# Expert rows of 8 KB, fetched token rows, and one square root per group of queries

## The chip, the core and the metric

The kernel runs on one core of a Trainium2 chip. TensorE multiplies matrices from SBUF into PSUM, VectorE, ScalarE and GpSimd do the elementwise work, SyncE issues most DMAs, and 16 DMA engines carry the bytes. The metric is device time in microseconds (us). The median of three runs of the kernel before is 1703.13 us.

## What is computed

One layer of a diffusion backbone over 512 latent tokens and 256 context tokens, width 1024, in float32: a modulated normalisation, three token mixers in parallel (a gated linear recurrence, a gated short convolution, and attention with normalised queries and keys), their merge into the stream x, and then a mixture of 16 experts in which every expert chooses its 64 best tokens.

```python
def attend_latent(q, k_lat, v_lat, k_ctx, v_ctx):   # 16 heads of 64 over 4 key heads
    ...
def expert_choice_ffn(h, router_w, w_gate, w_up, w_down):
    bsz, n, d = h.shape
    cap = CAPACITY_FACTOR * n // N_EXPERTS
    aff = jax.nn.softmax((h @ router_w).astype(jnp.float32), axis=-1)
    w_sel, idx = lax.top_k(aff.transpose(0, 2, 1), cap)
    xs = jax.vmap(lambda hb, ib: hb[ib])(h, idx)
    hid = jax.nn.silu(jnp.einsum('becd,edf->becf', xs, w_gate)) * jnp.einsum('becd,edf->becf', xs, w_up)
    ys = jnp.einsum('becf,efd->becd', hid, w_down) * w_sel[..., None].astype(h.dtype)
    return jax.vmap(lambda yb, ib: jnp.zeros((n, d), h.dtype).at[ib.reshape(-1)].add(yb.reshape(-1, d)))(ys, idx)
def reference(...):
    ...
    q_l = apply_rope(rmsnorm(to_heads(pl[8], HEAD_DIM), q_norm_g), cos, sin)
    ...
    x = x + g_a * y_lat
    x = x + g_f * expert_choice_ffn(modulate(x, norm2_g[l], sh_f, sc_f), router_w[l], w_gate[l], w_up[l], w_down[l])
    return rmsnorm(x, final_norm_g)
```

The three expert matrices are 1024 x 1024 each, so 16 experts have 192 MiB of weights, which are read once.

## The kernel before

Dense products take three passes with activations and weights split into a high and a low part (lines 185 to 187). A Tile scheduler orders most work by priorities and its own model of time; in the attention units SyncE and TensorE run in the order of the code, and in the expert stage TensorE does (`manual_schedule`).

**Attention.** Four groups of four query heads. `queries(g, w)` forms a group's queries in two halves of 256 tokens: three-pass products (`tok_steps`), a sum of squares, a square root on ScalarE (line 582), a reciprocal and a product on VectorE, the rotation (`rope`, VectorE and GpSimd) and a split. `turn_keys` (line 562) and `turn_queries` (line 599) turn keys and queries by transposes on TensorE. 64 units follow, 16 to a group: `scores`, an exponential on ScalarE (line 623), `turn_probs` (line 632) and `values` (line 647). Between them a `Filler` gives each unit a share of dense steps: the next group's queries, and convolution columns, through which `mixed` strews the query turns. The square root and the exponential need different tables on ScalarE.

**From merge to experts.** The last dense product (`w_out`, lines 883 to 905) makes x1, four tiles of 128 tokens x 1024, and the router logits from its transposes (line 875). The expert stage begins with top-k on VectorE. `slot` tells each token's place in each expert.

**Experts.** They go in eight pairs, expert e on rows 64 e to 64 e + 63 of a tile. `wsrc` lists the loads: 1 MiB each, 256 rows of a matrix as two rows of 4 KB on each partition; the last pair's down matrices come in column blocks (`LASTC`) with rows of 1 KB and 512 bytes. `more` issues them on SyncE. The first 24 go into the slots of `ORDER` while earlier stages give memory back; then a ring of 20 slots is refilled, each chunk of matmuls freeing two (`refill`). A pair runs: gate and up in eight chunks (`pair_chunks`, line 1099), Silu and product into `hid` (lines 1139, 1140), `gather` of the next pair's tokens as 32 matmuls with a scaled one-hot matrix (line 1048) with evictions through VectorE and ScalarE (lines 1053, 1051), `weights` (line 1062), `scatter` of the pair before into the accumulator (lines 1085 to 1090), transposes of hid (line 1153), `by_slot` (line 1073), and four chunks of down. In the last pair the column blocks (line 1194) are added to x1 and normalised as they come.

## Time and profile before

| | |
|---|---|
| median of three runs | 1703.13 us (1701.49 to 1704.36) |
| profiled execution | 1698.42 us |
| its span | 1696.6 us |
| TensorE busy in the span | 1607.2 us (95%) |
| VectorE, ScalarE, GpSimd busy | 767.9, 527.7, 150.7 us |
| DMA | 305.52 MB, 180 GB/s in the mean |
| chain that ended last | TensorE 83%, VectorE 9%, ScalarE 5% |

Roughly: recurrence until 430 us, convolution, keys and values until 540, attention units until 815, merge and router until 1213, experts until the end. A busy TensorE is one with instructions in flight. All stretches are in us from the start of the span.

### The profile page before, as it was taken

To read this page: it belongs to the slowest core of one execution; us is meant where nothing else is said; L and a number is where in the kernel's file an instruction comes from. 1 tells how busy PE (TensorE), PEld (TensorE's weight loads), DVE (VectorE), ACT (ScalarE), POOL (GpSimd) and SP (SyncE) were. 2 spreads that over 40 slices of the span, in tenths; PEclk is the share of its full clock that TensorE was granted. 3 is DMA by queue.
4 is the path that set the end of the run, shared out by engine and by line. 5 is a ranking of instruction groups with operands and counts; after the bars stand their busy time and mean duration, and the time that the engine had idled before them with its cause. 6 is when DMAs were issued, how large, how long until landed. Compare 5 with 4: busy or idle time off the path is not lost.

```text
span 1696.6 us, 23600 instructions
## 1 busy us (share of the span) xinstructions
PE 1607.2 (95%) x9896; PEld 1207.7 (71%) x9896; DVE 767.9 (45%) x1173; ACT 527.7 (31%) x934; POOL 150.7 (9%) x142
## 2 busy tenths in 40 slices
PE   6999999999998899899999999999799999999996
PEld 4889898988898788788788888889244344444444
DVE  6364655556545666655646524343411222122124
ACT  4433324334225656654323223233010010011004
POOL 0021212222000000000000100110000000000005
PEclk9999999999999999999999999999899999999998
DMA  9410211122222000100555622348789999999995
GB/s 294 118 41 25 63 38 50 38 75 70 80 80 75 26 25 26 44 33 26 182 191 178 209 85 75 124 148 349 315 320 402 382 409 409 409 409 409 409 395 167
DMA packets 166287, 305.52 MB, mean 180 GB/s; under 512 B 6562, under 2 KB 115618, under 8 KB 164130
## 3 DMA queue, kind: packets, MB, share of 16 engines
q1 hardware_dynamic: 162624, 301.66, 48.9%
q10 hardware_dynamic: 3556, 2.35, 0.4%
q8 instruction: 78, 1.28, 0.3%
q14 instruction: 29, 0.24, 0.0%
HBM read 301.89 MB, written 2.10 MB: 179 GB/s over the span
## 4 chain that ended last, share of the span: by engine, by line
PE 83%; DVE 9%; ACT 5%; issue 2%; POOL 0%; DMA 0%; ACTq 0%; SPq 0%; DVEq 0%; POOLq 0%
PE d L185 14%; PE d L187 14%; PE d L186 14%; PE pg L1099 6%; PE pu L1099 6%; PE py L1099 6%; PE py L1048 3%; PE lv L304 2%; PE tp L647 2%; PE tp L632 2%; DVE wl L91 1%; PE mi L333 1%; PE sc L617 1%; PE sc L618 1%; ACT wh L90 1%
## 5 line engine op out<-in xcount | busy, mean ns | idle before, releaser
L185 PE MATMUL d<-hH,wh 128*128 128x512 f32 x640 | 257.2, 402 | 0.0
L187 PE MATMUL d<-hH,wl 128*128 128x512 f32 x640 | 253.4, 396 | 0.0
L186 PE MATMUL d<-hL,wh 128*128 128x512 f32 x640 | 252.4, 394 | 0.0
L91 DVE TENSOR_TENSOR wl<-raw,wh 128x2048 fp32r<-128x2048 f32 (+1 forms) x78 | 157.8, 2022 | 192.0 <-ACT wh L90 191.8
L90 ACT ACTIVATE wh<-raw 128x2048 fp32r<-128x2048 f32 (+1 forms) x78 | 128.9, 1652 | 218.2 <-PE d L186 167.4
L187 PEld LDWEIGHTS d<-hH,wl 128*128 128x128 f32 x640 | 121.0, 189 | 24.9
L185 PEld LDWEIGHTS d<-hH,wh 128*128 128x128 f32 x640 | 120.8, 189 | 22.3 <-issue 1.6
L186 PEld LDWEIGHTS d<-hL,wh 128*128 128x128 f32 x640 | 121.1, 189 | 21.3 <-issue 0.2
L1099 PE MATMUL pg<-mw,xT 128*64 128x512 f32 x512 | 115.6, 593 | 2.0 <-DVE xT L1053 2.0
L1099 PE MATMUL pu<-mw,xT 128*64 128x512 f32 x512 | 115.3, 592 | 0.0
L1099 PE MATMUL py<-mw,hT 128*64 128x512 f32 x448 | 97.7, 594 | 0.1
L315 POOL TENSOR_TENSOR kk<-kk,tt 128x384 f32<-128x384 f32 x56 | 77.0, 1376 | 190.8 <-DVE tt L317 143.6
L1099 PEld LDWEIGHTS pu<-mw,xT 128*64 128x64 f32 x512 | 36.7, 137 | 73.1 <-issue 72.8
L1099 PEld LDWEIGHTS pg<-mw,xT 128*64 128x64 f32 x512 | 36.1, 137 | 72.2 <-issue 68.8
L185 PE MATMUL d<-wh,hH 128*128 128x256 f32 x288 | 84.1, 292 | 0.0
L187 PE MATMUL d<-wh,hL 128*128 128x256 f32 x288 | 81.7, 284 | 0.0
L186 PE MATMUL d<-wl,hH 128*128 128x256 f32 x288 | 81.6, 283 | 0.0
L1140 DVE TENSOR_TENSOR hid<-hid,pu 128x1024 f32<-128x1024 f32 x8 | 9.8, 1221 | 154.4 <-PE pu L1099 148.0
L187 PE MATMUL d<-brh,wl 128*128 128x512 f32 x192 | 75.6, 396 | 2.6 <-DVE wl L91 2.6
L185 PE MATMUL d<-brh,wh 128*128 128x512 f32 x192 | 75.8, 396 | 1.7 <-ACT wh L90 1.5
L186 PE MATMUL d<-brl,wh 128*128 128x512 f32 x192 | 75.7, 396 | 0.0
L1099 PEld LDWEIGHTS py<-mw,hT 128*64 128x64 f32 x448 | 31.5, 137 | 60.8 <-issue 59.7
(354 smaller groups left out, 2998.1 us busy)
## 6 DMA issues: line engine op xcount, KB each, us to landing
mw<-in_w_gate_dram SPq DMA_DIRECT2D x64, 1024.0 KB, 18.2
mw<-in_w_up_dram SPq DMA_DIRECT2D x64, 1024.0 KB, 18.5
mw<-in_w_down_dram SPq DMA_DIRECT2D x62, 1024.0 KB, 17.4
raw<-in_w_in_dram SPq DMA_DIRECT2D x38, 1024.0 KB, 5.1
raw<-in_ada_w_dram SPq DMA_DIRECT2D x16, 1024.0 KB, 4.9
raw<-in_w_in_dram SPq DMA_DIRECT2D x24, 512.0 KB, 3.8
adaw<-in_ada_w_dram SPq DMA_DIRECT2D x8, 512.0 KB, 8.5
raw<-in_ada_w_dram SPq DMA_DIRECT2D x8, 512.0 KB, 7.8
```

The source lines that it names most:

```text
L90: act.activation(hi, src, AF.Copy)
L91: dve.tensor_sub(lo, src, hi)
L185: pe.matmul(p, lh(k), rh(k), start=k == 0, stop=False)
L186: pe.matmul(p, lh(k), rl(k), start=False, stop=False)
L187: pe.matmul(p, ll(k), rh(k), start=False, stop=k == KC - 1)
L304: pe.matmul(p[:, c], kc[:, c * 128:(c + 1) * 128], q_mix, start=True, stop=True)
L315: pool.tensor_mul(kb[:, :, 1], kb[:, :, 1], tb[:, :, 0, 0:1].to_broadcast([128, n2, m]))
L333: pe.matmul(pv[:, i], kt[:, i], v[:, c], start=True, stop=True)
L632: pe.transpose(tp[:, t], e[:, (t0 + t) * 128:(t0 + t + 1) * 128], ident)
L647: pe.matmul(av[hh * 64:hh * 64 + 64, i], va[:, t, g * 64:g * 64 + 64], pts[hh][:, t], start=t == 0, stop=t == 5)
L1048: pe.matmul(p[:, i], x1[:, t, (k0 + i) * 128:(k0 + i + 1) * 128], ohs[:, t], start=t == 0, stop=t == 3)
L1099: pe.matmul(dst[64 * e:64 * e + 64, hf_], src[:, k, 64 * e:64 * e + 64], wt[e][:, k2, hf_ * 512:hf_ * 512 + 512], start=k == 0, stop=k == ...
```

## The change

Six things change.

- **Expert rows.** A gate, up or down load (all but the last pair's column blocks) puts two neighbouring matrix rows on one partition, one run of 8 KB instead of two of 4 KB. The contracted index is thereby interleaved, so everything that multiplies it takes columns with a step of two (`every2`): transposes of hid and of x1, the router's rows, the second norm's vectors.
- **Fetched rows.** x1 is written to a DRAM tensor `xd` by four DMAs on SyncE. From pair 2 on, `weights(pr)` also yields each slot's token number and 1/rms from two more columns beside the affinities (`facts`); `fetch` reads the 128 rows by an indirect DMA of GpSimd and scales them on VectorE, and `turn_rows` turns them by eight transposes. Pairs 0 and 1 still gather by matmuls (`pick`).
- **Order in a pair.** `turn_rows` of the next pair comes ahead of Silu; scatter comes behind the transposes of hid; `weights`, `by_slot` and one-hot run one to two pairs ahead.
- **One square root per group.** Sums of squares of both halves go into one tile, and one square root and one reciprocal serve both.
- **Turns in a line.** Key and query turns go into a list, `aside`; each unit takes one, unless a division is owed.
- **Filler items.** A convolution column pair is cut into `early_part` and `later_part` around the queries' turn. This raises the planned total, and so the share of a unit.

```diff
+    def every2(v, k):
+
+        o = k // 2 * 256 + k % 2
+        return v[:, o:o + 255:2]
...
-        qsps[g] = []
+        qsps[g], qfs = [], []
+        ssq = at.tile([128, 2, 2, 4], F32, name="ssq", bufs=2)
...
+        aside.extend([lambda i=i: turn_keys(i) for i in range(4)])
         for half in range(2):
             p = ps.tile([128, 2, 256], F32, name="d")
-            n = 0
             for i in range(2):
                 for _ in tok_steps(w, 2 + 2 * half + i, p[:, i]):
                     yield 1
-                    n += 1
-                    if half and n % 4 == 0:
-                        turn_keys(n // 4 - 1)
-                        yield 0.5
-            qf = at.tile([128, 2, 4, 64], F32, name="qf")
+            qf = at.tile([128, 2, 4, 64], F32, name="qf", bufs=2)
+            qfs.append(qf)
             act.activation(qf.rearrange("p t h d -> p t (h d)"), p, AF.Copy)
             sq = at.tile([128, 2, 4, 64], F32, name="qsq")
             act.activation(sq.rearrange("p t h d -> p t (h d)"), p, AF.Square)
-            ssq = at.tile([128, 2, 4], F32, name="ssq", bufs=2)
-            dve.tensor_reduce(ssq, sq, axis=AX.X, op=OP.add)
-            act.activation(ssq, ssq, AF.Sqrt, scale=1.0 / 64, bias=eps)
-            dve.reciprocal(ssq, ssq)
-            dve.tensor_mul(qf, qf, ssq[:, :, :, None].to_broadcast([128, 2, 4, 64]))
+            dve.tensor_reduce(ssq[:, half], sq, axis=AX.X, op=OP.add)
+        act.activation(ssq, ssq, AF.Sqrt, scale=1.0 / 64, bias=eps)
+        dve.reciprocal(ssq, ssq)
+        for half, qf in enumerate(qfs):
+            dve.tensor_mul(qf, qf, ssq[:, half, :, :, None].to_broadcast([128, 2, 4, 64]))
...
     def turn_queries(g):
         qst = at.tile([128, 4, S], F32R, name="qst", bufs=2)
-        for half, qsp in enumerate(qsps.pop(g)):
-            for hp in range(2):
-                p = psc.tile([128, 4, 128], F32R, name="tp")
-                for h2 in range(2):
-                    for t in range(2):
-                        pe.transpose(p[:, 2 * h2 + t], qsp[:, t, 2 * hp + h2], identr)
-                act.activation(qst[:, 2 * hp:2 * hp + 2, half * 256:half * 256 + 256],
-                               p.rearrange("p (h t) c -> p h (t c)", t=2).bitcast(F32), AF.Copy)
-                yield 0.7
-        qsts[g] = qst
-
-    qsps = {}
+
+        def turn(half, hp):
+            p = psc.tile([128, 4, 128], F32R, name="tp")
+            for h2 in range(2):
+                for t in range(2):
+                    pe.transpose(p[:, 2 * h2 + t], qsps[g][half][:, t, 2 * hp + h2], identr)
+            act.activation(qst[:, 2 * hp:2 * hp + 2, half * 256:half * 256 + 256],
+                           p.rearrange("p (h t) c -> p h (t c)", t=2).bitcast(F32), AF.Copy)
+            if half and hp:
+                qsts[g] = qst
+
+        aside.extend([lambda i=i: turn(i // 2, i % 2) for i in range(4)])
+        return iter(())
+
+    qsps, aside = {}, []
...
-    def mixed(c, turn):
-
-        def steps(w):
-            t = turn()
-            n = 0
-            for cost in c[1](w):
-                yield cost
-                n += 1
-                if n % 3 == 0:
-                    yield next(t, 0.0)
-            yield from t
-        return c[0], steps
+    parts = []
+
+    def early_part(c, w):
+
+        it = c[1](w)
+        parts.append(it)
+        for _ in range(KC):
+            yield next(it)
+
+    def later_part():
+        yield from parts.pop()
...
     mm0, turn0 = q_items(0)
-    Filler([mm0, c2[0], turn0]).drain()
+    first = Filler([mm0, c2[0], turn0])
+    first.fill(33)
+    for _ in range(4):
+        first.fill(4)
+        aside.pop(0)()
+    first.drain()
+    for _ in range(4):
+        aside.pop(0)()
     fill_items = []
...
         mm, turn = q_items(g)
-        fill_items += [mm, mixed(c, turn[1])]
+        fill_items += [mm, (c[0], lambda w, c=c: early_part(c, w)), turn, (None, later_part)]
     fl = Filler(fill_items + c3[1:])
...
             core(turn_probs, u)
             if u + 2 < len(units):
                 while units[u + 2][0] not in qsts:
+                    if aside:
+                        aside.pop(0)()
                     fl.fill(1)
                 core(scores, u + 2)
             fl.fill(share / 2)
-            while owed:
+            if owed:
                 owed.pop()()
+            elif aside:
+                aside.pop(0)()
+                fl.fill(1)
...
+    facts = xp.tile([128, 4, NE + 2], F32, name="aff")
+    aff = facts[:, :, :NE]
+    dram, dram_e = opn("xd", space=bass.MemoryType.DRAM)
+    xd = dram.tile([S, D], F32, name="xd")
 
...
-                pe.transpose(tp[:, kk, i], x1[:, t + i, j2 * 256 + kk * 128:j2 * 256 + kk * 128 + 128], ident)
+                pe.transpose(tp[:, kk, i], every2(x1[:, t + i], 2 * j2 + kk), ident)
...
     partial_logits(*pend.pop())
+    for t in range(4):
+        sp.dma_start(xd[t * 128:(t + 1) * 128], x1[:, t])
     dve.tensor_reduce(ss2, ssp, axis=AX.X, op=OP.add)
     act.activation(ss2, ss2, AF.Sqrt, scale=1.0 / D, bias=eps)
     dve.reciprocal(ss2, ss2)
+    pool.tensor_copy(facts[:, :, NE:NE + 1], iota[:, 64:68, None])
+    pool.tensor_copy(facts[:, :, NE + 1:NE + 2], ss2[:, :, None])
...
-                wsrc += [mat[e, kk * 256:kk * 256 + 256].rearrange("(a p) f -> p a f", p=128) for e in pair]
+                wsrc += [mat[e, kk * 256:kk * 256 + 256].rearrange("(p a) f -> p (a f)", p=128) for e in pair]
...
-                wsrc += [w_down[e, kk * 256:kk * 256 + 256].rearrange("(a p) f -> p a f", p=128) for e in pair]
+                wsrc += [w_down[e, kk * 256:kk * 256 + 256].rearrange("(p a) f -> p (a f)", p=128) for e in pair]
...
+    def scaled(pr):
+
         ohs = ma.tile([128, 4, 2 * CAP], F32, name="ohs")
-        dve.tensor_mul(ohs, ohf, ss2[:, :, None].to_broadcast([128, 4, 2 * CAP]))
...
+    def evict(xT, p, k, on_act):
+        if on_act:
+            act.activation(xT[:, k], p, AF.Identity, scale=ab2[:, 0, k:k + 1], bias=ab2[:, 1, k:k + 1])
+        else:
+            dve.tensor_scalar(xT[:, k], p, ab2[:, 0, k:k + 1], ab2[:, 1, k:k + 1], op0=OP.mult, op1=OP.add)
...
+    def pick(pr, k0, p, on_act):
+
+        xT, ohs = xs[pr]
         n = p.shape[1]
...
-                pe.matmul(p[:, i], x1[:, t, (k0 + i) * 128:(k0 + i + 1) * 128], ohs[:, t], start=t == 0, stop=t == 3)
...
+                pe.matmul(p[:, i], every2(x1[:, t], k0 + i), ohs[:, t], start=t == 0, stop=t == 3)
+        for i in range(n):
+            evict(xT, p[:, i], k0 + i, on_act)
+
+    def fetch(pr):
+
+        xg = mb.tile([128, D], F32, name="hid")
+        pool.indirect_dma_start(xg, None, xd, bass.IndirectOffsetOnAxis(ap=which.pop(pr), axis=0))
+        dve.tensor_scalar(xg, xg, norm[:, pr:pr + 1], None, op0=OP.mult)
+        fetched[pr] = xg
+
+    def turn_rows(pr):
+
+        xg = fetched.pop(pr)
+        p = pm.tile([128, 2, 4, 128], F32, name="py")
+        xT = ma.tile([128, KC, 2 * CAP], F32, name="xT")
+        for k in range(KC):
+            pe.transpose(p[:, k // 4, k % 4], every2(xg, k), ident)
+        for k in range(4):
+            evict(xT, p[:, 0, k], k, False)
+            evict(xT, p[:, 1, k], k + 4, True)
+        xs[pr] = xT, None
...
         ohf = hot[pr][1]
-        pw = ps.tile([128, NE], F32, name="d")
+        pw = ps.tile([128, NE + 2], F32, name="d")
         for t in range(4):
-            pe.matmul(pw, ohf[:, t], aff[:, t], start=t == 0, stop=t == 3)
+            pe.matmul(pw, ohf[:, t], facts[:, t], start=t == 0, stop=t == 3)
+        if pr > 1:
+            which[pr] = sm.tile([128, 1], mybir.dt.uint32, name="which", bufs=2)
+            dve.tensor_copy(which[pr], pw[:, NE:NE + 1])
+            dve.tensor_copy(norm[:, pr:pr + 1], pw[:, NE + 1:NE + 2])
         for e in range(2):
...
+            if pr == 1 and kk == 0:
+                weights(2)
+                fetch(2)
...
+        if 0 < pr and not last:
+            turn_rows(pr + 1)
         hid = mb.tile([128, D], F32, name="hid")
         act.activation(hid, pg.rearrange("p a b -> p (a b)"), AF.Silu)
         dve.tensor_mul(hid, hid, pu.rearrange("p a b -> p (a b)"))
-        if not last:
+        if pr == 0:
+            scaled(1)
             pn = pm.tile([128, 2, 4, 128], F32, name="py")
-            gather(pr + 1, 0, pn[:, 0], False)
-            gather(pr + 1, 4, pn[:, 1], True)
-            weights(pr)
-        if not last and waiting:
-            scatter(*waiting, 2, lambda t: pm.tile([128, 2, 512], F32, name=("pg", "pu")[t // 2]))
+            pick(1, 0, pn[:, 0], False)
+            pick(1, 4, pn[:, 1], True)
+            weights(0)
+            weights(1)
+        elif pr + 2 < NE // 2:
+            weights(pr + 2)
         hT = mb.tile([128, KC, 128], F32, name="hT")
         for h4 in range(2):
             tp = ps.tile([128, 4, 128], F32, name="d")
             for i in range(4):
                 k = 4 * h4 + i
-                pe.transpose(tp[:, i], hid[:, k * 128:(k + 1) * 128], ident)
+                pe.transpose(tp[:, i], (hid[:, k * 128:(k + 1) * 128] if last else every2(hid, k)), ident)
             act.activation(hT[:, 4 * h4:4 * h4 + 4], tp, AF.Copy)
-        if 0 < pr < NE // 2 - 1:
-            oT_t = by_slot(pr)
-            if pr + 2 < NE // 2:
-                one_hot(pr + 2)
+        if not last and waiting:
+            scatter(*waiting, 2, lambda t: pm.tile([128, 2, 512], F32, name=("pg", "pu")[t // 2]))
+            turned[pr + 1] = by_slot(pr + 1)
+            if pr + 3 < NE // 2:
+                one_hot(pr + 3)
         py = pm.tile([128, 2, 512], F32, name="py")
         if last:
...
-            oT_t = by_slot(0)
+            for i in range(2):
+                turned[i] = by_slot(i)
             one_hot(2)
...
+        waiting = pr, turned.pop(pr), yH, yL
+        if 0 < pr < NE // 2 - 2:
+            fetch(pr + 2)
+
+
+    oT_t = turned.pop(pr)
```

SyncE, the first 24 expert loads (`mw`), with what each waits for; `x_8633` is x1. Before:

```order
L962 DMA mw<-in_w_gate_dram 128x2x1024 [waits DMAHW7_49]
L962 DMA mw<-in_w_down_dram 128x2x1024 [waits DMAHW0_49]
L962 DMA mw<-in_w_up_dram 128x2x1024 [waits DMAHW1_49,DVE_49]
L962 DMA mw<-in_w_up_dram 128x2x1024 [waits DMAHW2_49,DVE_49]
L962 DMA mw<-in_w_gate_dram 128x2x1024 [waits DMAHW3_49,PE_49]
L962 DMA mw<-in_w_gate_dram 128x2x1024 [waits DMAHW4_49]
L962 DMA mw<-in_w_up_dram 128x2x1024 [waits DMAHW5_49,DVE_49]
```

and now:

```order
L988 DMA mw<-in_w_gate_dram 128x2048 [waits DMAHW7_49]
L988 DMA mw<-in_w_down_dram 128x2048 [waits DMAHW0_49]
L928 DMA xd<-x_8633 128x1024 [waits DMAHW1_49,DVE_49]
L928 DMA xd<-x_8633 128x1024 [waits DMAHW2_49]
L988 DMA mw<-in_w_up_dram 128x2048 [waits DMAHW3_49,Activation_49]
L928 DMA xd<-x_8633 128x1024 [waits DMAHW4_49,DVE_49]
L928 DMA xd<-x_8633 128x1024 [waits DMAHW5_49]
L988 DMA mw<-in_w_up_dram 128x2048 [waits DMAHW6_49,Activation_49]
L988 DMA mw<-in_w_gate_dram 128x2048 [waits DMAHW7_49,PE_49]
```

The four writes of x1 stand behind the 11th load, ahead of the 12th and of the 13th to 24th.

TensorE, from the last up chunk of a middle pair to its scatter; `ident` marks a transpose. Before:

```order
L1099 MATMUL pu<-mw,xT 64x512 x8
L1048 MATMUL py<-ohs,x_8645 128x128 x32
L1062 MATMUL d<-aff,oh 128x16 x4
L1085 MATMUL pg<-hT,ohT 128x512
L1086 MATMUL pg<-yL,ohT 128x512
```

and now:

```order
L1152 MATMUL pu<-mw,xT 64x512 x8
L1099 MATMUL py<-ident,hid 128x128 x8
L1111 MATMUL d<-aff,oh 128x18 x4
L1213 MATMUL d<-ident,hid 128x128 x8
L1138 MATMUL pg<-hT,ohT 128x512
L1139 MATMUL pg<-yL,ohT 128x512
```

The 32 gather matmuls are gone, eight transposes of fetched rows and eight of hid stand there, and the scatter (lines 1138, 1139) moved behind them.

ScalarE, the second half of a group's queries among attention units (`e` is the exponential, `pt` the turned probabilities, `spl` the split queries). Before, where such a piece stands twice in a group:

```order
L623 ACTIVATE e,den<-sc,mx 128x768
L582 ACT_TABLE_LOAD
L582 ACTIVATE ssq<-ssq,eps 128x8
L636 ACTIVATE pt<-tp 128x512
L623 ACT_TABLE_LOAD
L623 ACTIVATE e,den<-sc,mx 128x768
L90 ACTIVATE spl<-qsq 128x8x64
```

and now, once in a group:

```order
L629 ACTIVATE e,den<-sc,mx 128x768
L642 ACTIVATE pt<-tp 128x512
L584 ACT_TABLE_LOAD
L584 ACTIVATE ssq<-ssq,eps 128x16
L629 ACT_TABLE_LOAD
L629 ACTIVATE e,den<-sc,mx 128x768
```

The square root takes both halves' sums (128x16), and one pair of table loads in a group is gone.

## Rows read from the trace of the kernel before

**Rows 1.** The page: busy time by engine, and GB/s in 40 slices of 42.4 us

```profile
PE 1607.2 (95%) x9896; PEld 1207.7 (71%) x9896; DVE 767.9 (45%) x1173; ACT 527.7 (31%) x934; POOL 150.7 (9%) x142
...
GB/s 294 118 41 25 63 38 50 38 75 70 80 80 75 26 25 26 44 33 26 182 191 178 209 85 75 124 148 349 315 320 402 382 409 409 409 409 409 409 395 167
```

**Rows 2.** Chain of waits, pair 2 (start us, us, what)

```profile
1334.34 3.43 PE pg L1099 x16
...
1361.81 3.78 PE py L1048 x32
1365.61 1.38 DVE xT L1053 x4
1367.03 3.84 PE py L1048 x32
...
1377.99 13.88 PE py L1099 x64
1391.88 3.43 PE pg L1099 x16
```

**Rows 3.** DMA, stretches 1219-1266, 1266-1326, 1326-1600 and 1643-1675 us, one line each

```profile
DMA packets 4081, 15.75 MB, mean 335 GB/s; under 512 B 240, under 2 KB 240, under 8 KB 4080
...
DMA packets 5739, 22.17 MB, mean 370 GB/s; under 512 B 336, under 2 KB 336, under 8 KB 5735
...
DMA packets 29030, 112.09 MB, mean 409 GB/s; under 512 B 1701, under 2 KB 1701, under 8 KB 29016
...
DMA packets 10524, 8.90 MB, mean 278 GB/s; under 512 B 175, under 2 KB 10402, under 8 KB 10521
```

**Rows 4.** DMA, 894.8-896.4 us (adaLN rows of 8 KB) and 1646-1660 us (1 KB rows)

```profile
DMA packets 82, 0.67 MB, mean 420 GB/s; under 512 B 0, under 2 KB 0, under 8 KB 0
...
DMA packets 4822, 4.88 MB, mean 349 GB/s; under 512 B 71, under 2 KB 4821, under 8 KB 4821
```

**Rows 5.** SyncE's queue 1100-1330 us (start, us, issues), and VectorE at 1187 us

```profile
1172.92 0.88 SPq L962 DMA_DIRECT2D mw<-in_w_gate_dram  x2
1187.61 0.88 SPq L962 DMA_DIRECT2D mw<-in_w_up_dram  x2
1188.54 8.29 SPq L962 DMA_DIRECT2D mw<-in_w_down_dram  x7
1218.94 1.23 SPq L962 DMA_DIRECT2D mw<-in_w_gate_dram  x2
...
1187.61 0.69 DVE L896 TENSOR_TENSOR x<-xt,xr 128x512 f32<-128x512 f32 x1
```

**Rows 6.** Timeline of the last pair's middle, by engine (start us, us, instruction)

```profile
1657.82 1.03 ACT L1139 ACTIVATE hid<-pg 128x1024 f32<-128x1024 f32 x1 [3.00 <-PE pg L1099]
...
1661.87 1.22 DVE L1140 TENSOR_TENSOR hid<-hid,pu 128x1024 f32<-128x1024 f32 x1
...
1663.15 1.09 PE L1153 MATMUL d<-ident,hid 128*128 128x128 f32 x8 [1.94 <-DVE hid L1140]
...
1680.49 1.97 PE L1194 MATMUL pg<-mw,hT 128*64 128x128 f32 x32
```

**Rows 7.** DMA, GB/s of 1660-1680 us in slices of 0.5 us

```profile
GB/s 346 346 336 325 321 304 288 325 290 207 229 283 288 305 261 166 266 323 273 186 109 29 0 0 0 0 0 0 0 0 0 0 0 0 0 0 0 0 0 0
```

**Rows 8.** Windows in attention: us, busy PE, PEld, DVE, ACT, POOL, clock, DMA

```profile
560.00:600.00 40.00, 34.94 (x291) 30.26 (x291) 25.89 (x45) 26.77 (x49) 3.26 (x4) 0.96 0.08 27
...
620.00:660.00 40.00, 35.83 (x321) 31.82 (x315) 26.78 (x42) 26.59 (x47) 3.58 (x4) 1.00 0.09 27
...
680.00:740.00 60.00, 53.71 (x486) 47.34 (x484) 34.66 (x56) 35.58 (x63) 3.59 (x4) 1.00 0.11 36
740.00:803.00 63.00, 62.89 (x490) 52.90 (x490) 38.34 (x59) 31.21 (x56) 0.13 (x2) 1.00 0.10 35
```

**Rows 9.** Line 582 on ScalarE: table loads, ns min/median/max, first and last start

```profile
L582 ACT ACT_TABLE_LOAD  x6: 1283/1283/1283, 563.3 to 716.6; - x6
```

**Rows 10.** The page: issues of expert weights, xcount, KB each, us to landing

```profile
mw<-in_w_gate_dram SPq DMA_DIRECT2D x64, 1024.0 KB, 18.2
```

More of the change, by code (lines that the diff above doesn't have):

```diff
@@ L720, in body, with column @@
     accs = {}
-    def column(src, put):
+    def column(src, put, at_k=lambda v, k: v[:, k * 128:(k + 1) * 128]):
         p = pl.tile([128, KC], F32, name="tp")
         for k in range(KC):
-            pe.matmul(p[:, k:k + 1], src[:, k * 128:(k + 1) * 128], ones[:, 0:1], start=True, stop=True)
+            pe.matmul(p[:, k:k + 1], at_k(src, k), ones[:, 0:1], start=True, stop=True)
         put(p)
@@ L746, in ada_more @@
                 later.append(lambda: gate_rows(lo))
-                later.append(lambda: column(hi, lambda p: dve.tensor_copy(ab2[:, 1], p)))
+                later.append(lambda: column(hi, lambda p: dve.tensor_copy(ab2[:, 1], p), every2))
             else:
                 later.append(lambda: column(lo, lambda p: dve.scalar_tensor_tensor(ab2[:, 0], p, 1.0, vecs[:, 1],
-                                                                                  op0=OP.add, op1=OP.mult)))
+                                                                                  op0=OP.add, op1=OP.mult), every2))
                 later.append(lambda: column(hi, lambda p: dve.tensor_copy(gfc, p)))
@@ L962, in more @@
             sp.dma_start(t, src)
+            if len(src.shape) == 2:
+                t = t.rearrange("p (a f) -> p a f", a=2)
             loaded.append(t)
@@ L1023, in body @@
     pm, pm_e = opn("pm", space=PSUM, bufs=1)
-    xs = {}
-    hot = {}
+    xs, hot, which, fetched = {}, {}, {}, {}
     def one_hot(pr):
@@ L1047, in gather @@
             for t in range(4):
-                pe.matmul(p[:, i], x1[:, t, (k0 + i) * 128:(k0 + i + 1) * 128], ohs[:, t], start=t == 0, stop=t == 3)
-        for k in range(k0, k0 + n):
-            if on_act:
-                act.activation(xT[:, k], p[:, k - k0], AF.Identity, scale=ab2[:, 0, k:k + 1], bias=ab2[:, 1, k:k + 1])
-            else:
-                dve.tensor_scalar(xT[:, k], p[:, k - k0], ab2[:, 0, k:k + 1], ab2[:, 1, k:k + 1], op0=OP.mult,
-                                  op1=OP.add)
+                pe.matmul(p[:, i], every2(x1[:, t], k0 + i), ohs[:, t], start=t == 0, stop=t == 3)
[16 more added lines that the diff above has]
+        xs[pr] = xT, None
     def weights(pr):
@@ L1103, in early @@
     def early(k0):
-        gather(0, k0, ps.tile([128, 2, 128], F32, name="d"), False)
+        pick(0, k0, ps.tile([128, 2, 128], F32, name="d"), False)
     with tc.manual_schedule(engines={mybir.EngineType.DVE}):
         one_hot(0)
+        scaled(0)
         early(0)
+    turned = {}
     waiting = None
@@ L1257, in layout @@
     a["w_out"] = f["w_out"][0]
-    a["router"] = f["router_w"][0].reshape(8, 128, 16).transpose(1, 0, 2)
+    a["router"] = f["router_w"][0].reshape(4, 128, 2, 16).transpose(1, 0, 2, 3).reshape(128, 8, 16)
     a["w_gate"] = f["w_gate"][0]
```

26 lines of the change are left out of this document (11 added, 15 removed).

## Prediction

> **What bounds the kernel now.** I read the page first for where the time lies: TensorE is busy 95% of the span, and from slice 33 the DMA engines move a flat 409 GB/s [rows 1]. So in the expert stage, from about 1213 us on, two resources are nearly full, and the question is which wait ends last. The chain of waits answers it: in pair 2 it never leaves TensorE and its evictions. From 1334.34 to 1391.88 one pair takes 57.5 us: 27.5 us of gate and up, then 16.2 us between 1361.81 and 1377.99, of which two gathers and the eviction between them are 3.78 + 1.38 + 3.84 = 9.0 us, then 13.9 us of down [rows 2]. Nowhere in it does TensorE wait for a load.
>
> The DMA view then tells how far off the loads are. After the first refill at 1218.94 [rows 5] 168 loads are left: 160 of 1 MiB in 4 KB rows and 8 MiB of narrow column blocks. At 409 GB/s a 1 MiB load takes 2.564 us, so 160 take 410 us; the narrow ones take 27 us, 1643.9 to 1671. That is 437 of the 452 us until the last bytes at about 1671 [rows 3, 7], and the missing 15 us are idle time early on: 15.75 MB in 47 us and 22.17 MB in 60 us are 8.5 and 5.8 us short of 409 GB/s [rows 3]. TensorE starts the last column block at 1680.5 [rows 6], 9.5 us after its bytes are there. So the stage is bound by TensorE with the loads right behind it. Whatever shortens only TensorE's pair by more than some 10 us in total runs into the loads.
>
> In attention TensorE is the bound too, with holes: it is idle 5.1, 4.2 and 6.3 us in the three stretches in which a group's queries are normalised, and 0.1 us in the 63 us behind them [rows 8].
>
> **The change part by part.** All sums are against the profiled execution, 1698.42 us with a span of 1696.6; the runs shown have a median of 1703.13, 4.7 us above it, and I apply the difference in us to that median.
>
> *Rows fetched, not gathered.* Pairs 2 to 7 lose the 32 gather matmuls and their eviction wait, 9.0 us each [rows 2]. They gain eight transposes, and what lay under the gather comes into the open: in the order TensorE has only 8 transposes and 4 small matmuls ahead of the transposes of hid, which need 1.03 us of ScalarE and 1.22 us of VectorE [rows 6]. I take 0.7 + 1.03 + 1.22 = 2.9 us, and the middle falls from 16.2 to 10.1 us, a pair from 57.5 to 51.4. Six pairs give 36.6 us, so TensorE alone would end at about 1660. Per pair the loads need 24 x 2.50 = 60 us even at the faster rate below. TensorE is therefore 9 us a pair too fast, and the stage's end must be made up from the loads.
>
> *8 KB rows.* The trace holds 8 KB rows already: in the middle of one adaLN load, with nothing else moving, they go at 420 GB/s; 1 KB rows go at 349 [rows 4] and 4 KB rows at 409 [rows 3]. A line through the per-packet times of 1 and 4 KB (46.9 and 160.2 ns over 16 engines) gives 311 ns for 8 KB, 421 GB/s, the same. I take 420: 2.497 us a load. Below, the bound is 409 (nothing); above, 430 (twice the gain), since the 420 is read from only 1.6 us.
>
> The Trainium skill ("DMA: Bandwidth & Descriptors", section "Why small descriptors are slow (HBM only)") gives a fixed overhead of about 3 cycles of 32 bytes a packet. By it 8 KB rows would gain 1.2%, 414 GB/s as an estimate, and the sum would end 7 us later than mine, at 1689 us. This trace has a larger step already between 1 and 4 KB (17% where the page's figure makes 7%), so the measured rates decide.
>
> *The copy of x1 to DRAM.* Four writes, 2.1 MB, stand in SyncE's queue behind the 11th expert load, and the second two wait for the last x1 rows, which VectorE finishes at 1188.3 [rows 5]. Queued behind them are the 13th to 24th load, of which the 13th to 15th were out by 1173.8 until now [rows 5]. Nobody on TensorE waits for that: the last of pair 0's gate and up loads have landed by 1206, and its fourth quarter begins around 1244. But the loads run later: 1188.5 + 2.6 (1.05 MB of writes) + 12 x 2.497 = 1221.1 for the 24th, 2 us behind the first refill, where until now the engines idled at 1211 to 1219.
>
> *The fetches.* Six gathers of 512 KB by GpSimd add 3.1 MB, 7.5 us of the loads' time at 420 GB/s. The page of the profile has no DMA issued from GpSimd, so their latency is bounded: below by the bytes alone, 1.2 us; above by a load that queues behind its fellows, 18.2 us in the median [rows 10]. The first is issued behind the first quarter of pair 1's gate and up, the others some 3 us into the gate and up of a pair; all are read behind the last quarter, at least 20 us later. I cost the wait at nothing, these matmuls being the cover.
>
> *Strided reads.* Columns are now taken with a step of two in TensorE's weight loads (32 router transposes, 64 transposes of hid and 48 of fetched rows, 64 picks). No row shows a strided weight load; I take no cost. If one cost double, the 32 router transposes, the only ones on a path that ends last besides pair 0, and pair 0's picks would cost some 4 us each, so up to 8. Below nothing I exclude, as the reads don't shrink.
>
> *The sum for experts.* 1221.1 + 160 x 2.497 (399.5) + 7.5 + 27 for the narrow blocks, unchanged, + idle time. Of the 14.3 us [rows 3] I keep 10: pair 0's pick for pair 1 stays, the hole of pair 1 shrinks because slots come free 6 us sooner; bounds 5 and 15. The last bytes land at 1665.1. From the start of the last column block to the end it took 1696.6 - 1680.5 = 16.1 us [rows 6], a chain of small steps that is not touched: 1681.2, or **15.4 us** less.
>
> *Attention.* The table loads at line 582 fall from 6 to 3, each 1.283 us [rows 9] with another back to the exponential behind it: 7.7 us of ScalarE, each pair of them in the chain that made the holes. Half of the 15.6 us of holes goes, 7.8. Against it: VectorE's rope of both halves now comes in one burst in front of the row maxima, and in the order the filler ends at unit 53 of 64, where it now fills a stretch that has no holes [rows 8]. The scheduler pulls gate matmuls into that gap; I charge 3 us. Net **5 us**, between 11 less and 3 more. All work behind it shifts with it, TensorE being the bound up to the experts.
>
> Together 20.4 us: a span of 1676.2, an execution of 1678.0, and 1703.1 - 20.4 = **1682.7 us** against the median.
>
> **The rivals.** *Rows no faster.* If the 8 KB rows stay at 409, 172 loads x 0.067 us = 11.5 us of the gain go; 1694 us. For it: 1.6 us of trace is thin, and the 4 KB rows are already near what 8 KB rows reach. Against: 1, 4 and 8 KB lie on one line. 13%.
>
> *TensorE's clock.* The chain is now one in which TensorE waits about 1.5 us in every 5 us. In attention the clock fell in one of the three stretches with holes (0.96 in the mean), and not in the full one [rows 8]. If the granted clock falls to 1.2 GHz in the last pair, its column blocks take 7 us against 6 us of loading and its last gate and up 3.4 us more, some 10 us in all; 1693 us. Earlier pairs don't matter, 20 slots of buffer lie between. 10%.
>
> *Fetches too late (slower).* VectorE scales the fetched rows in line ahead of the weights' copies and the product for hid, and TensorE's eight transposes wait for it. If a fetch takes L us, a pair can't be shorter than 2.9 + L + 1 + 10.1 + 13.9. The loads make a pair 61.2 us; with the gain of 20.4 spread over five pairs the change turns slower from L = 37 us. At 45 us a pair takes 72.9, 5 x 11.7 = 58 us more in all: 1741. Against: it takes twice the 18.2 us of a load in a full queue. 6%.
>
> The Trainium skill ("SBUF — State Buffer", section "SBUF: two separate sides") speaks against the change here: a DMA issued from GpSimd gets no descriptors written while VectorE runs certain copies. No run here shows it, and VectorE's copies are far shorter than the cover.
>
> *Strided weight loads cost double*, or the attention order loses what the square roots give: 1690, 6%.
>
> **How the numbers follow.** The forecast has the remaining 65%, by itself from 1668 (430 GB/s on 172 loads, 10 us less, and attention 5 better) to 1695 (idle 15, half the rate's gain). All rivals but the slow one lie in or at that range; 1668 to 1697 leaves out the late fetches and tails on both sides. About 0.2%, 3.4 us, is what a measurement can tell from no change. Faster than 1699.7 are the forecast, most of the first two rivals and the last: 0.88; within 0.2%: 0.06; slower: 0.06.
>
> **What would show it.** Right: in the expert stage the DMA rate flat at about 420 from 1226 on, chain and waits of TensorE naming loads of mw in pairs 3 to 7, the middle of a pair at some 10 us, the last bytes near 1660 (with attention's 5 us), three table loads for ssq in groups 1 to 3. Wrong: no waits of TensorE for loads (then my rate or bytes are off), a rate of 409, or waits of VectorE for a fetch. A gain beyond 35 us would mean that 8 KB rows are much faster than the one load shows.

## The result and the profile after

The changed kernel took 1682.6 us (median of 4 runs, 1680.8 to 1683.9) beside 1702.8 us of the kernel before: a ratio of 0.988, 95% interval 0.986 to 0.990. A second comparison with more runs (6 and 11, last experiment below) gave 1685.1 beside 1702.0, 0.990 (0.988 to 0.992). So the medians differ by 17 to 20 us, and the forecast of 1682.7 with 20.4 us lies at the upper edge of that. The stages below hold only 13 to 16 us of it.

The profiled execution took 1683.86 us. From its page, TensorE's share, GB/s in 40 slices, and the fetches' own queue; the flat rate is 419 to 420 GB/s where [rows 1] had 409.

```profile
PE 1581.5 (94%) x9560; PEld 1179.9 (70%) x9560; DVE 766.0 (46%) x1181; ACT 520.4 (31%) x924; POOL 156.4 (9%) x150
...
GB/s 287 119 50 26 63 29 61 37 53 75 76 85 86 11 51 51 26 51 1 178 198 175 200 97 80 125 102 299 393 357 368 419 419 419 419 420 419 420 415 229
...
q0 software_dynamic: 864, 3.15, 0.5%
```

The chain of waits answers [rows 2] (start us, us, what). In pair 2 the middle is 1356.19 to 1366.74, 10.55 us instead of 16.2. Then the chain leaves TensorE: from 1374 to 1580 it follows load behind load, ten of some 20 us each. At 1579.85, behind the last up load of pair 6, it goes back to TensorE, and stays with it and with the steps of VectorE and ScalarE between its matmuls for 102 us, to the end.

```profile
1352.76 3.43 PE pu L1152 x16
1356.19 1.16 PE py L1099 x8
...
1359.95 1.23 PE d L1213 x8
1362.14 1.23 DVE moe L1143
1366.74 7.07 PE py L1152 x32
1374.20 20.86 DMA mw<-in_w_up_dram
...
1559.91 19.90 DMA mw<-in_w_up_dram
1579.85 3.65 PE pu L1152 x14
```

What TensorE waited for after 1180 us (us in total, times, longest): loads now have rows, 11 us in 8 waits together. The kernel before has none.

```profile
PE pu L1152 <- DMA mw<-in_w_up_dram: 7.2, 5, 1.9
...
PE pg L1152 <- DMA mw<-in_w_gate_dram: 4.0, 3, 1.3
```

DMA of the changed kernel, three stretches: 1255.5 to 1264 us (a hole), 1280 to 1630 (nothing but 8 KB rows), and 1630 to 1670 in slices of 1 us, where the last bytes land at about 1664.2.

```profile
DMA packets 29, 0.14 MB, mean 16 GB/s; under 512 B 13, under 2 KB 13, under 8 KB 13
...
DMA packets 20566, 146.77 MB, mean 419 GB/s; under 512 B 2279, under 2 KB 2279, under 8 KB 3047
...
GB/s 451 410 418 410 418 428 386 380 361 343 347 351 347 348 348 347 349 347 347 349 348 349 357 337 334 311 290 295 236 302 240 259 250 122 18 0 0 0 0 0
```

SyncE's queue around the hole (start us, us, issues): the 24th load goes out at about 1199; the second load of 1247.41 then waits until 1263.4 for a slot, which only pair 0's first down chunk gives back. The last row, from SyncE's waits in 1100 to 1680 us (us in total, times, longest), names the down products (`py`, line 1152) as what ended it.

```profile
1176.67 0.81 SPq L928 DMA_DIRECT2D xd<-x  x2
...
1188.87 10.51 SPq L988 DMA_DIRECT2D mw<-in_w_down_dram  x7
...
1247.41 15.96 SPq L988 DMA_DIRECT2D mw<-in_w_up_dram  x2
1263.45 18.52 SPq L988 DMA_DIRECT2D mw<-in_w_down_dram  x8
...
SPq L988 <- PE py L1152: 48.5, 11, 15.2
```

The fetches of pairs 3 to 7 (issues, us to landing), VectorE's waits for all six (us in total, times, longest), and the start of the last column block on TensorE:

```profile
hid<-xd,which POOLq DMA_INDIRECT x5, 8.6
...
DVE hid L1090 <- DMA hid<-xd,which: 58.8, 6, 10.6
```

```profile
1666.00 1.97 PE L1260 MATMUL pg<-mw,hT 128*64 128x128 f32 x32
```

Attention's windows, answering [rows 8] (us, busy PE, PEld, DVE, ACT, POOL, clock, DMA): TensorE's idle time in the three stretches fell from 15.6 to 5.2 us, and grew by some 5 us in the stretches between and behind them.

```profile
560.00:600.00 40.00, 38.75 (x317) 34.20 (x316) 28.06 (x48) 25.16 (x46) 3.42 (x6) 1.00 0.09 27
...
620.00:660.00 40.00, 39.15 (x343) 34.48 (x339) 25.96 (x45) 23.98 (x42) 3.44 (x4) 1.00 0.08 27
...
680.00:740.00 60.00, 56.88 (x448) 48.49 (x448) 37.12 (x56) 34.19 (x60) 3.40 (x6) 1.00 0.11 36
```

**By stages.** For every kernel below, from the first and last start of a line's matmuls, in us: where the attention units begin (first `scores`), how long they last (to the last `values`), where pair 0 begins, and how long the experts take (to the last matmul of the last column block). Median and runs are of the comparison that the kernel was in.

| kernel | begins | units | pair 0 | experts | median (runs) |
|---|---|---|---|---|---|
| before | 540.7 | 264.8 | 1215.3 | 466.9 | 1702.8 (4) |
| before, second profile | 541.2 | 266.3 | 1216.5 | 467.0 | 1701.9 (10) |
| changed | 542.2 | 258.5 | 1210.9 | 456.8 | 1682.6 (4) |
| changed, second profile | 545.2 | 258.7 | 1215.3 | 456.7 | 1685.1 (6) |
| rows of 4 KB | 545.4 | 258.8 | 1214.8 | 464.9 | 1692.2 (4) |
| no fetched rows | 541.1 | 258.5 | 1209.5 | 473.0 | 1699.1 (10) |
| x1 written from ScalarE | 542.2 | 258.8 | 1212.1 | 457.6 | 1684.8 (4) |
| fetches left out | 542.4 | 258.8 | 1211.7 | 449.8 | 1677.7 (4) |
| attention as before | 540.0 | 267.2 | 1218.4 | 457.9 | 1691.8 (6) |
| one square root alone | 543.1 | 281.1 | 1235.1 | 456.9 | 1708.2 (8) |
| line alone | 547.0 | 263.0 | 1218.8 | 456.7 | 1685.7 (6) |
| smaller share | 542.9 | 259.7 | 1213.0 | 457.0 | 1686.1 (5) |
| pair 1 fetched | 541.2 | 258.7 | 1210.0 | 454.9 | 1681.3 (4) |
| the same, Silu early | 541.9 | 258.7 | 1211.0 | 453.9 | 1681.2 (5) |

The stages repeat within 1 or 2 us; the beginning does not, and the section on the prediction says where it varies. Experts give 10 us. The units give 6 to 8, but what lies between them and pair 0 is 0.4 to 2.4 us longer, and they begin some 1 us later.

### The profile page after: what moved, and what is told of

The parts are those of the page before. It is cut to its first block, busy times and chain, and to the rows that moved or that the text cites. A ratio compares the mean times of both kernels' runs of the same rounds, so it can differ in the third digit from the quotient of the medians.

```text
span 1682.1 us, 22948 instructions
## 1 busy us (share of the span) xinstructions
PE 1581.5 (94%) x9560; PEld 1179.9 (70%) x9560; DVE 766.0 (46%) x1181; ACT 520.4 (31%) x924; POOL 156.4 (9%) x150
## 3 DMA queue, kind: packets, MB, share of 16 engines
q8 instruction: 75, 1.23, 0.3%
## 4 chain that ended last, share of the span: by engine, by line
PE 46%; DMA 12%; DVE 5%; ACT 3%; issue 1%; ACTq 0%; SPq 0%; DVEq 0%
DMA mw<-in_w_up_dram 9%; PE d L190 8%; PE d L192 8%; PE d L191 8%; DMA mw<-in_w_down_dram 4%; PE pu L1152 3%; PE pg L1152 3%; PE py L1152 3%; PE tp L653 2%; PE tp L638 2%; PE sc L623 1%; PE sc L624 1%; DVE wl L91 1%; ACT wh L90 1%; ACT e L629 1%
## 5 line engine op out<-in xcount | busy, mean ns | idle before, releaser
L1152 PE MATMUL pu<-mw,xT 128*64 128x512 f32 x512 | 120.6, 593 | 7.2 <-DMA mw<-in_w_up_dram 7.2
L1152 PE MATMUL pg<-mw,xT 128*64 128x512 f32 x512 | 120.0, 595 | 6.2 <-DMA mw<-in_w_gate_dram 4.0
L1152 PEld LDWEIGHTS py<-mw,hT 128*64 128x64 f32 x448 | 31.5, 137 | 60.6 <-issue 59.7
L629 ACT ACTIVATE e<-sc,mx 128x768 f32<-128x768 f32 x64 | 57.6, 901 | 43.3 <-DVE mx L627 43.0
```

The costliest lines, as they stand in the source:

```text
L629: act.activation(e, pf, AF.Exp, bias=mx, accum_out=dens[g, hp][:, qt, hh:hh + 1])
L1152: pe.matmul(dst[64 * e:64 * e + 64, hf_], src[:, k, 64 * e:64 * e + 64], wt[e][:, k2, hf_ * 512:hf_ * 512 + 512], start=k == 0, stop=k == ...
```

## The experiments

The medians of the kernel before, beside which the kernels were run, were 1701.3 us for the first four, 1702.2 for the three on attention and for fetch1, 1701.2 for share, fetch1s and the kernel before again, and 1702.0 for the changed kernel again.

**Rows of 4 KB** (label rows4k). The whole of that part is undone: the loads, and with them the step of two.

```diff
-        o = k // 2 * 256 + k % 2
-        return v[:, o:o + 255:2]
+        return v[:, k * 128:(k + 1) * 128]
...
-    wsrc += [mat[e, kk * 256:kk * 256 + 256].rearrange("(p a) f -> p (a f)", p=128) for e in pair]
+    wsrc += [mat[e, kk * 256:kk * 256 + 256].rearrange("(a p) f -> p a f", p=128) for e in pair]
```

> The changed kernel with the expert rows of before (4 KB, no step of two in the columns); fetched rows and attention stay. Theory L (the loads bound the experts until the last up load of pair 6 at 1579.9 us, TensorE has 102 us of its own behind that): the 160th load comes 136 x 0.06 us later, 8 us, and 1 us more in the first 24, so 1691 to 1693 us, with a rate of 409 GB/s and more and longer waits of TensorE for loads. Rival T (TensorE sets the end, the waits for loads are incidental): at most 2 us more, 1683 to 1685.

1692.2 us, and 8.1 us more in the experts. DMA from 1326 to 1580 us, and TensorE's waits for loads, 19 us where the changed kernel has 11:

```profile
DMA packets 26957, 103.89 MB, mean 409 GB/s; under 512 B 1624, under 2 KB 1624, under 8 KB 26945
```

```profile
PE pu L1151 <- DMA mw<-in_w_up_dram: 11.6, 9, 1.9
PE pg L1151 <- DMA mw<-in_w_gate_dram: 7.7, 6, 1.5
```

The loads set the pace until the last ones; theory L holds. With fetched rows but rows of 4 KB the experts are only 2 us shorter than before (464.9 against 466.9).

**No fetched rows** (pick_all): every pair gathers again, where the turn of the fetched rows stood.

```diff
-            turn_rows(pr + 1)
+            pn = pm.tile([128, 2, 4, 128], F32, name="py")
+            pick(pr + 1, 0, pn[:, 0], False)
+            pick(pr + 1, 4, pn[:, 1], True)
```

> The changed kernel without fetches and without the copy of x1: every pair gathers by 32 matmuls where the turn of the fetched rows stood; 8 KB rows, the new order in a pair and attention stay. Theory L: a pair is TensorE-bound again at 57 to 58 us, no waits for loads after pair 1, only attention's part of the gain stays: 1696 to 1700 us. Rival R (the 8 KB rows carry the gain, the fetch adds little): 1685 to 1689.

1699.1 us. TensorE waits for no load. A pair takes 58.5 us (chain of waits, one middle):

```profile
1360.08 3.98 PE py L1080 x32
1364.08 1.38 DVE xT L1072 x4
1365.50 4.04 PE py L1080 x32
1369.54 0.80 PE d L1109 x8
1372.66 1.23 DVE moe L1141
1377.27 13.88 PE py L1150 x64
```

The 8 KB rows alone give nothing while TensorE is the bound: the experts are 6 us longer than before. Each of the two parts is worth little without the other; together they give 10. The pair is 1 us longer than before. The gathers take 3.98 and 4.04 us instead of 3.78 and 3.84 [rows 2], which is the price of the step of two. The rest of the 1 us goes with the new order: all eight transposes of hid now stand in the chain (from 1370.34 to 1371.69), where before four stood there for 0.45 us. Eight in a row took 1.03 us before (pair 2) and take 1.23 with the step, as the chain of the changed kernel above has it:

```profile
1376.16 1.03 PE L1153 MATMUL d<-ident,hid 128*128 128x128 f32 x8
```

**x1 written from ScalarE's queue** (xd_act).

```diff
-        sp.dma_start(xd[t * 128:(t + 1) * 128], x1[:, t])
+        act.dma_start(xd[t * 128:(t + 1) * 128], x1[:, t])
```

> The changed kernel with the four writes of x1 issued by ScalarE's queue, so that SyncE's 12th to 24th load no longer stand behind them. By the prediction's sum, which starts at the landing of the 24th load, the 13th to 15th load go out some 10 us earlier and 7 us are won: 1675 to 1677. By the hole theory (the DMA engines stood idle from 1255 to 1264 us because no slot of the ring was free, so earlier loads only make that hole longer) nothing is won: 1681 to 1684.

1684.8 us, nothing won. Four loads did go out 15 to 23 us earlier (from 1160.23 and 1169.87; 1177.57 to 1187 in the changed kernel), but the slot wait ends where it did, 52.6 us after pair 0's begin in both:

```profile
1160.23 1.88 SPq L988 DMA_DIRECT2D mw<-in_w_up_dram  x2
1169.87 0.90 SPq L988 DMA_DIRECT2D mw<-in_w_gate_dram  x2
...
1248.67 15.95 SPq L988 DMA_DIRECT2D mw<-in_w_up_dram  x2
1264.72 3.82 SPq L988 DMA_DIRECT2D mw<-in_w_down_dram  x3
```

**Fetches left out** (nofetch).

```diff
-        pool.indirect_dma_start(xg, None, xd, bass.IndirectOffsetOnAxis(ap=which.pop(pr), axis=0))
+        pool.memset(xg, 1.0)
```

> The six fetches are left out: GpSimd fills the tile with ones, so pairs 2 to 7 compute on wrong tokens; the copy of x1, the scaling and the turns stay. Theory L: 3.15 MB less in the loads' stream at 419 GB/s, 7.5 us: 1674 to 1677. Rival H (the fetches find room beside the loads, or the time is TensorE's): 1681 to 1684.

1677.7 us, and 7.0 us less in the experts: the bytes of the fetches are on the path, at nearly their full price of 7.5.

**Attention as before** (attn_old), **one square root alone** (sqrt_only) and **the line alone** (line_only), each with the experts of the changed kernel. The second is the first with the two halves' sums in one tile; the third is the changed kernel with a square root in each half, and the diff is a part of its.

```diff
-            dve.tensor_reduce(ssq[:, half], sq, axis=AX.X, op=OP.add)
-        act.activation(ssq, ssq, AF.Sqrt, scale=1.0 / 64, bias=eps)
...
+            ssq = at.tile([128, 2, 4], F32, name="ssq", bufs=2)
+            dve.tensor_reduce(ssq, sq, axis=AX.X, op=OP.add)
+            act.activation(ssq, ssq, AF.Sqrt, scale=1.0 / 64, bias=eps)
```

> The changed kernel with attention as before (two square roots a group, turns strewn through the products). Theory S: all behind attention comes 4.4 to 6 us later, the loads too, since the last first loads wait for x1 and the ring for pair 0: 1687 to 1689 us, last attention product near 805 us in its profile (800.7 in the changed kernel's, 805.5 before). Rival A: the loads absorb it, 1682 to 1684.

> The changed kernel with the turns and the filler of before, but one square root per group. Theory S (the table loads made the holes): the holes of TensorE from 560 to 740 us fall from 15.6 to about 8, three table loads for ssq in groups 1 to 3, and 3 to 5 us of attention's gain are here: 1683 to 1685. Rival T (the turns, which stood as a block behind the products, made them): 1686 to 1688 us, holes as before.

> The changed kernel with turns in a line and the cut filler, but two square roots a group. Theory S: six table loads for ssq, holes of 12 us or more, 0 to 2 us of gain left: 1686 to 1688. Rival T: most of the gain is here, 1683 to 1685.

1691.8, 1708.2 and 1685.7 us; units of 267.2, 281.1 and 263.0 us against 258.6 with both. None of the three medians lies in a range that was set for it. Neither theory holds by itself: one square root by itself costs 14 us of the units; the line by itself gives 2 to 4, and the square root gives 4 more only behind the line. TensorE's longest sum of waits in 540 to 830 us, of one square root alone, of the line alone and of the kernel before:

```profile
PE tp L606 <- DVE spl L91: 24.1, 3, 10.1
```

```profile
PE tp L636 <- ACT pt L640: 6.9, 7, 2.1
```

```profile
PE tp L632 <- ACT pt L636: 11.5, 7, 3.1
```

With one root the split queries of both halves come only behind the second half, and the turns of before stand three convolution steps behind it: TensorE, whose order is fixed, waits 24 us for them, three times in the kernel. The line puts the whole early part of a convolution pair in between, and no such wait is left.

**A smaller share of filler** (share).

```diff
-        share = fl.total() / len(units)
+        share = (fl.total() - 42) / len(units)
```

> The changed kernel with a smaller share of filler for each unit of attention: the planned total less 42 (18 for the added items, 24 for the steps that go with the turns in the line), so that the filler lasts for all 64 units. The prediction charged 3 us to its end at unit 53. Theory F: the wait of 6.1 us for ScalarE's split weights at about 805 us and the idle time behind it go, 2 to 4 us: 1679 to 1681. Rival: gate products of the next stage already fill that stretch, 1681.5 to 1684; or the turns now come too late and it is 1684 to 1688.

1686.1 us, no gain, and in the range that was given for turns that come too late. The wait it was aimed at did shrink, from the first row (changed kernel) to the second (smaller share), but TensorE's idle time in 560 to 600 and 620 to 660 us grew by 3.2 us, the units became 1 us longer and pair 0 began no earlier. The 3 us that the prediction charged for the filler's early end are not to be had there.

```profile
PE d L190 <- ACT wh L90: 6.1, 1, 6.1
```

```profile
PE d L190 <- ACT wh L90: 1.5, 1, 1.5
```

**Pair 1 fetched too** (fetch1), and the same with Silu's table loaded early and two idle matmuls (fetch1s).

```diff
+            if pr == 0 and kk == 1:
+                for e in once["a"][::-1]:
+                    e.close()
+                mb, _ = opn("mb", reuse_waits="tile")
+                weights(1)
+                fetch(1)
...
-            scaled(1)
-            pn = pm.tile([128, 2, 4, 128], F32, name="py")
-            pick(1, 0, pn[:, 0], False)
-            pick(1, 4, pn[:, 1], True)
```

> The changed kernel with pair 1 fetched too: its one-hot and weights come behind the first quarter of pair 0, the first slot that becomes the fetch's tile is used four loads earlier, and pair 0's two gathers for pair 1 (9.5 us from 1247 to 1256.4) go. Hole theory: pair 0's down products begin some 7 us earlier, so the ring's slots come free 7 us earlier, the idle time of the DMA engines from 1255 to 1264 us shrinks to 2 us or less, and against one more fetch (1.25 us) 5 to 6 us are won: 1676 to 1678. Rival: the tail (TensorE from 1580 us on, 102 us) or the fetch's latency on pair 0 takes it back: 1681 to 1684.

> The kernel with pair 1 fetched, with two additions: an idle Silu of one column ahead of pair 0 loads ScalarE's table early (it stood with 1.28 us in the chain at 1248.25), and two matmuls without use stand between the weights and the transposes of hid, where TensorE waited 2.9 us and the granted clock fell to 0.50 (1252 to 1258 us). Pair 0's down products should begin 1.3 us earlier and run at full clock from the start, so the ring's slots come free 2.5 to 3 us earlier than in the kernel with pair 1 fetched: 1678 to 1680 us. If the loads' idle time is not what is left there: 1681 to 1682.

1681.3 and 1681.2 us: by the medians both lie in the ranges that were set for no gain. The experts are 1.9 and 2.9 us shorter, right in sign, a third to a half of what the hole theory promised. Pair 0's middle fell from 12.4 us to 8.0 and 6.9. But behind it the granted clock fell to the lower level, 1.2 GHz (first row: the window 1252 to 1258 of pair 1 fetched), and pair 0's down took 15.8 us instead of 13.95 (second row; third row: the changed kernel), so that the slots came free at 1260.9, 50.9 us after the pair's begin instead of 52.6.

```profile
1252.00:1258.00 6.00, 4.88 (x16) 2.46 (x18) 0.97 (x3) 2.34 (x5) 0.00 (x0) 0.50 0.79 332
```

```profile
1254.98 15.76 PE py L1158 x64
```

```profile
1259.36 13.95 PE py L1152 x64
```

These have the lowest medians of the kernels that leave nothing out, but by less than the runs can tell from the changed kernel.

**The kernel before and the changed kernel again** (before_again, after_again).

> The kernel before, unchanged, for a second profile of it. The medians differ by 20.2 us, the two profiles by 14.5 (attention and what lies ahead of it 4.4, experts 10.1), since the profiled execution of before was 4.3 us under its median. Theory V (the first 540 us and attention vary from run to run, the expert stage doesn't): pair 0 to the last column block takes 466 to 468 us again, and a span near 1700 shows the rest ahead of the experts. Rival E (the expert stage was short in that profile): 470 us or more.

> The changed kernel, unchanged, for more runs beside the kernel before and a second profile. The profiles so far give 16 us: experts 10 (467 to 457 us from pair 0 to the last column block, in both profiles of before), attention units 7 (265 to 267 against 258.6), the start of attention 1 to 1.5 later. If that is the whole effect, the medians of many runs differ by 15 to 17 us, and the 20.2 came from few runs. If the effect is 20, they differ by 18.5 or more, and the profile should show a stage of before or after that the first two profiles caught at an unusual length.

1701.9 us (10 runs) and 1685.1 (6). The stages repeat: 467.0 and 456.7 us of experts, 266.3 and 258.7 of units. The first dense product starts at 56.5 and 56.9 us in the two profiles of before, and at 56.8 and 59.7 us in those of the changed kernel; from there to the end of the span it is 1640.1 and 1640.9 us, and 1625.3 and 1626.6. So 13.5 to 15.6 us are the effect as far as it can be located, 10 of them in the experts. The medians differ by 16.9 us in this comparison and by 20.2 in the first, and no profile shows where the rest lies.

## Why the prediction came out

**Right by its steps.** The bound moved from TensorE to the loads, as the sum assumed: chain and waits above show it, and so do the runs that change the loads alone (rows of 4 KB cost 8.1 us, the fetches' bytes 7.0, both in the experts). The rate was 419 GB/s, forecast 420, and 2.4% above the 409 of 4 KB rows. The Trainium skill ("DMA: Bandwidth & Descriptors", section "Why small descriptors are slow (HBM only)") gives a fixed overhead of about 3 cycles a packet beside one for every 32 bytes, by which an estimate is 1.2%: the trace has twice that. A pair's middle came to 10.55 us (10.1), fetches landed in 8.6 us (the first in 10.0), inside the bounds of 1.2 to 18.2 and far below the 37 at which they would have decided. VectorE did wait for each of them, up to 10.6 us, which the prediction had listed as a sign of being wrong; but TensorE waited for none, and nothing on the chain stood behind these waits. The narrow blocks took 27 us (27). Attention was forecast at 5 us net: from the begin of the units to pair 0 it is 674.6 and 675.3 us before, 668.7 and 670.1 after, and the units begin about 1 us later, so it gave 4 to 5. Its two terms were both too small: the holes shrank by 10.4 us instead of 7.8, and the charge against it was nearer 5 us than 3.

**The term that was mis-sized.** Experts gained 10.1 us, not 15.4. Counted from x1, the last bytes came 3.5 us later than the sum had them (1664.2; 1665.1 less the 4.4 us by which all ahead had shifted is 1660.7): idle time of 11.5 us instead of 10 (9.3 us of missing bytes in 1226 to 1266, 2.2 in 1266 to 1326), 0.9 us of the rate, and some 1.2 us of a ragged start of the stream at 1184 to 1190 (1.99 MB in 6 us). And the last column block did not follow its bytes: it began at 1666.0, 1.8 us behind them, because TensorE's 102 us from 1579.85 on were by then the longer of the two. The sum had treated the end as a matter of the loads alone, where both arrive together. 3.5 and 1.8 make the 5.3.

How close the two are, the line alone shows. Pair 6's middle took 11.9 us in the changed kernel and 10.4 there, because the granted clock was 0.86 in the first (1583.5 to 1595.4 us, a mean of its two levels) and 1.00 in the second; the transposes of hid, changed kernel first:

```profile
1587.07 1.98 PE d L1213 x8
```

```profile
1595.30 1.22 PE d L1211 x8
```

Yet the experts took the same 456.7 us. With the faster middle TensorE waited for the bytes of the third column block, and the last one still began 1.4 us behind its own:

```profile
PE pu L1258 <- DMA mw<-in_w_down_dram: 0.4, 1, 0.4
```

**A step that was wrong though its sum was not.** The sum began at the landing of the 24th load. Writing x1 from another queue sent four loads 15 to 23 us earlier and won nothing: what the loads wait for is pair 0's first down chunk on TensorE, and everything ahead of it only makes the hole longer. "Nobody on TensorE waits for that" was right of the copy, and should have been said of the later ones of the first loads too. So the rate was not flat from 1226 us on, as the prediction had it: the engines stood nearly still from 1255.5 to 1264.

**Attention for half of the reason.** The forecast gave the whole gain to the table loads. They did go from 6 to 3, and behind the line one square root a group is worth 4 us of the units, though no run parts the table loads from the other work that goes with a second root. But alone, without the line, it loses 14 us, because the turns of before come too soon in TensorE's fixed order for queries that are split so late. The prediction listed VectorE's burst, but not what stood queued behind the later queries. Of a diff with the square root alone it would have had the sign wrong.

**The rivals.** Rows no faster: excluded by 419 GB/s. The clock in the last pair: its column blocks ran at the granted clock of 1.00 in 1650 to 1670 us; in 1580 to 1600, in pair 6's middle, it was 0.91, and behind pair 0 it took a part of the gain of the kernel with pair 1 fetched, so the mechanism was real, at other places. Strided weight loads: not double, but not free, see below. The slow fetch did not occur. Two figures beside the forecast are off: by the Trainium skill's overhead the sum would end 6 us later, not 7, and the two terms named for the upper end (idle 15, half the rate's gain) make 1693.4, not 1695.

**The median, and luck.** That 1682.7 was met by 1682.6 is luck. Of the 20.4 us the stages hold about 14.5: 10 of 15.4 in the experts, 4 to 5 of 5 in attention. The difference was applied to a median of three runs, 1703.1; over 10 to 15 runs the kernel before has 1701.2 to 1702.2, and the changed kernel rose to 1685.1 in its second comparison. Much of the spread that the profiles show lies in the first 57 us, whose code the change leaves as it is: over all kernels here the first dense product starts at 55.6 to 61.7 us. The two profiles of the changed kernel differ by 4.2 us, 3.0 of them where the units begin (542.2 and 545.2), and their granted clock in 22 to 40 us was 0.91 and 0.72 (0.81 in the profile of before, the first row):

```profile
22.00:40.00 18.00, 14.73 (x130) 10.20 (x126) 14.61 (x35) 8.22 (x11) 0.00 (x0) 0.81 1.20 289
```

```profile
22.00:40.00 18.00, 14.23 (x126) 10.09 (x122) 14.69 (x36) 8.27 (x12) 0.00 (x0) 0.91 1.18 288
```

```profile
22.00:40.00 18.00, 14.65 (x105) 9.56 (x97) 12.03 (x28) 7.28 (x10) 0.00 (x0) 0.72 1.17 286
```

Why the clock holds longer in some executions than in others stays open, and so do the 2 to 6 us between the 14.5 us of the stages and the 16.9 and 20.2 of the medians.

## What to carry to other kernels

Where two resources end within 10 us of each other, work out when each is the bound and what hands over to the other, not one of them to the end: here loads until 1580 us, TensorE behind. A part that takes work off one resource can be worth nothing until the other is relieved too: measure the two changes apart and together. Before a gain is booked for loads that start earlier, look for the slot that they will wait for anyway. A step that makes an operand later (one root for two halves) is paid for by whatever stands behind it in a fixed order; move the consumer first, then merge the producer.

## What the runs showed that was not expected

A weight load with a step of two in fp32 costs half as much again. Weight loads of the transposes of x1 on TensorE (ns min/median/max), before and in the changed kernel:

```profile
L875 PEld LDWEIGHTS tp<-ident,x x32: 138/141/144, 1144.6 to 1188.8; 128*128 128x128 f32 x32
```

```profile
L896 PEld LDWEIGHTS tp<-ident,x x32: 193/208/214, 1139.8 to 1184.3; 128*128 128x128 f32 x32
```

With rows of 4 KB, and so without the step, the same loads are at 139 ns again. Most of it hides beside the matmuls: eight transposes take 1.23 us instead of 1.03, 32 gathers 4.0 instead of 3.8. The Trainium skill ("SBUF — State Buffer", section "Door 1: The DMA port swizzle (why `[64,N]` ≈ `[32,N]`)", box on SBUF cachelines) says that at least two hits in a line of 16 bytes are needed for the full bandwidth, and takes from it how far one can stride for free; by that a step of two in fp32, which has two hits in a line, would be free; the trace disagrees for weight loads, 208 against 141 ns.

TensorE's clock fell behind one short wait: with pair 1 fetched it waited 2.9 us for hid behind pair 0's gate and up, and the granted clock was 0.50, the level of 1.2 GHz, for the next 6 us. Two matmuls without use in that wait moved the fall from 1252 to 1256 us and made it shorter, behind a wait of 2.0 us for the last turned rows, but did not prevent it; pair 0's down took 15.7 us instead of 15.8. The window of the kernel with the two matmuls in which the clock is down:

```profile
1256.00:1258.00 2.00, 2.00 (x8) 0.49 (x4) 0.00 (x0) 0.00 (x0) 0.00 (x0) 0.50 0.82 344
```
